# Mamba-2 scan written feature-major, with the gate projected like every other tile

## Chip, core and metric

One core of one Trainium2 chip runs the whole program: two blocks of a small language model over 512 tokens. The metric is the time of one execution on the device in microseconds, here the median of three runs. Engines are called as in the profile: PE (TensorE, PEld its weight load), DVE (VectorE), ACT (ScalarE), POOL (GpSimd), SP (SyncE, which issues nearly all DMAs).

## What is computed

Two layers, each feed-forward half, mixer, feed-forward half. The mixer of the first layer is a Mamba-2 scan, of the second a sliding-window attention. All operands are fp32. The part that matters here, cut from the reference (32 heads of 64 in 8 groups of 4 heads, state 128, chunk 128, so 4 chunks):

```python
z, xbc, dt = split(u @ w_in)
xs, B, C = split(silu(causal_conv4(xbc) + conv_b))
dt = softplus(dt + dt_bias);  a_cum = cumsum(dt * a)          # within a chunk
decay = exp(where(causal, a_cum_l - a_cum_s, -inf))
y_diag = einsum('bclgn,bcsgn->bgcls', C, B) * decay  @  (xs * dt)
states = B^T @ (exp(a_end - a_cum) * xs * dt), carried over chunks with exp(a_end)
y = y_diag + (C @ states_before) * exp(a_cum) + d_skip * xs
gg = y * silu(z);  gg = gg * rsqrt(mean(gg * gg, over the 256 of a group) + eps)
out = (gg * norm_w) @ w_out
```

## The kernel before

**Layout.** Activations lie feature-major: 128 features on the partitions, 512 tokens along the row. A product of fp32 precision is made of three matmuls on halves (`mm3`, L326: high weight by high x, high by low, low by high). `project` (L331) makes one tile of 128 features by 512 tokens out of 8x3 such matmuls with 512 columns each. For every weight tile ACT casts the loaded `wraw` to `whi` (L218), and another engine subtracts to get `wlo` (L219): DVE, or POOL where `split_w` is given it. `next_w` (L225) splits two tiles ahead and loads four ahead; there are two buffers for `wraw` and four for each half.

**Mamba.** `mamba` (L459) runs through `MAMBA_ORDER` (L45), a hand-written list of tokens, once for each of 8 groups g: `z` the gate, `B`, `C`, `X`, `Y` projections with their convolution (`conv`, L521: one multiplication from PSUM into `xp`, one ACT and three DVE passes of 128x512 into `acc`, a Silu), `h` the decay factors, `a b c f g` the five steps of the generator `ssd` (L557), and `O` the output projection of an earlier group, whose 128x512 results DVE adds to the residual `h` (L455). The tokens of neighbouring groups are interleaved, and each engine executes its own instructions in the order that a scheduler made of the program. PSUM has four one-bank buffers (`mm`) and two two-bank buffers (`big`).

In this kernel y is token-major. `z_first` (L631) and `z_next` (L649) therefore hold x still and move the weights: 96 matmuls of 256 columns (288 in the first group, which carries the 32 columns of dt along). `steps` and `steps_end` (L480, L505) turn dt into the step sizes, their cumulated sums `acs` and the exponentials `ee`, and send the transposed sums to DRAM (`actr`). `decay` (L538) fetches them as rows over all partitions, and subtracts `acs` with 16 DVE instructions of 128x128 (L552) ahead of an Exp. In `ssd`, token c makes x token-major by 8 transposes (`psx`), copies it (L574), and scales it three ways: `xds` on DVE (L576), `xd` and `y` on POOL (L578, L580). Token f multiplies: `psy` 16 products of a 128x128 stationary factor with 64 columns of `xd` (L600), `pso` with the state (L603); then come four DVE passes over y (L604 to L607), squares with their row sums on ACT (L610), a reciprocal root by Newton's method on DVE (`rsqrt`, L293), and its product into y (L616). Token g transposes y back (`psyt`, L621) into the halves `ya`, `yb` that `O` multiplies.

Of the kernel before, what the change touches and what calls it, by code (L numbers as in the profile page):

```python
# [84 lines left out]
def weight_plan():  # L85
# [18 lines left out]
    def mamba():  # L104
# [6 lines left out]
        for tok in MAMBA_ORDER:  # L111
            s, g, q = parse(tok)
            z = np.arange(256) + g * 256
            if tok == "z0":
                zd = np.concatenate([z, 6144 + np.arange(32)])
                for ks in (range(0, 3), range(3, 6), range(6, 8)):
                    cols_over_k(wi, ks, zd)
            elif s == "z":
                for ks in (range(0, 4), range(4, 8)):
                    cols_over_k(wi, ks, z)  # L120
            elif s in "BCXY":
                c0 = {"B": 4096 + g * 128, "C": 5120 + g * 128, "X": 2048 + g * 256, "Y": 2176 + g * 256}[s]
# [795 lines left out]
```

## Time and profile before

| | |
|---|---|
| median of 3 runs (lowest, highest) | 2076.58 us (2074.08 to 2076.80) |
| the profiled execution, its own time | 2076.16 us |
| its span in the trace | 2074.4 us, so 1.8 us lie outside |
| busy share PE, DVE, ACT, POOL | 99%, 53%, 36%, 8% |
| mean granted PE clock | 0.998 |
| chain that ended last, share by engine | PE 91%, DVE 6%, ACT 1%, others under 1% each |
| Mamba stage | from 370 us (first `psz`) to about 820 us |

Busy time is the union of an engine's instructions; matmuls overlap in the pipeline, so that an instruction's duration is longer than its distance to the next, and the distance is what adds up. Where a timeline row has a count (x24), it is one uninterrupted run of instructions. A wait row names the engine that waited, what it was to execute, and whose instruction released it.

### The profile page before, as it was taken

The numbers are of one execution on the slowest core, as the hardware profiler recorded it, in microseconds if no ns is written. First come the engines' busy times: TensorE is split into PE (matmuls) and PEld (weight loads), VectorE is DVE, ScalarE is ACT, GpSimd is POOL, SyncE is SP. The second block draws the span as 40 slices with busy tenths as digits, with TensorE's granted clock in tenths as the row PEclk, the third lists the DMA queues.
The fourth block names the chain that finished last, engine by engine and source line by source line (L and its number), as shares of the span: only waits on it lengthen the run. The fifth ranks groups of instructions, "written<-read, shape, count | busy, mean of one in ns | idle before, by whom it ended". The sixth has DMA issues, their size and how long they took to land.

```text
span 2074.4 us, 24948 instructions
## 1 busy us (share of the span) xinstructions
PE 2045.5 (99%) x9991; PEld 1717.8 (83%) x9991; DVE 1093.8 (53%) x1782; ACT 736.7 (36%) x1088; POOL 166.1 (8%) x120
## 2 busy tenths in 40 slices
PE   8999999999999999999999999999999999999998
PEld 7888888888888887888888888888887788888887
DVE  6343433687888889434333346343338884443333
ACT  5232222445444444322222233232226563232231
POOL 0000001222222210000001000000102000000000
PEclk9999999999999999999999999999999999999999
DMA  5333232323333332233333333322332223333231
GB/s 172 102 92 102 87 104 87 114 92 91 94 100 102 102 102 72 92 102 92 101 94 92 99 100 98 102 92 94 99 102 62 62 71 92 96 97 101 89 98 69
DMA packets 58869, 197.64 MB, mean 95 GB/s; under 512 B 6656, under 2 KB 6912, under 8 KB 58752
## 3 DMA queue, kind: packets, MB, share of 16 engines
q1 hardware_dynamic: 58608, 196.03, 30.6%
q8 instruction: 79, 1.29, 0.3%
q14 instruction: 38, 0.31, 0.0%
q10 hardware_dynamic: 144, 0.00, 0.0%
HBM read 193.85 MB, written 2.16 MB: 94 GB/s over the span
## 4 chain that ended last, share of the span: by engine, by line
PE 91%; DVE 6%; ACT 1%; issue 1%; DMA 1%; POOL 0%; ACTq 0%; SPq 0%; DVEq 0%; POOLq 0%
PE mm L327 27%; PE mm L328 27%; PE mm L329 27%; PE psz L658 1%; PE psz L660 1%; PE psz L659 1%; PE psy L600 1%; DVE acc L528 1%; DVE wlo L219 1%; PE pav L799 0%; PE pp L788 0%; ACT lg L775 0%; POOL qkv L742 0%; PE pso L603 0%; DVE lg L768 0%
## 5 line engine op out<-in xcount | busy, mean ns | idle before, releaser
L218 ACT CAST whi<-wraw 128x1024 fp32r<-128x1024 f32 (+2 forms) x355 | 364.8, 1030 | 1061.0 <-PE mm L328 677.3
L327 PE MATMUL mm<-x,whi 128*128 128x512 f32 x1760 | 690.2, 392 | 5.8 <-DVE whi L216 5.8
L329 PE MATMUL mm<-x,wlo 128*128 128x512 f32 x1760 | 685.7, 390 | 0.9 <-DVE wlo L219 0.9
L328 PE MATMUL mm<-x,whi 128*128 128x512 f32 x1760 | 685.8, 390 | 0.0
L219 DVE TENSOR_TENSOR wlo<-wraw,whi 128x1024 fp32r<-128x1024 f32 (+3 forms) x329 | 392.1, 1192 | 305.8 <-ACT whi L218 291.7
L327 PEld LDWEIGHTS mm<-x,whi 128*128 128x128 f32 x1760 | 331.0, 188 | 74.9 <-ACT ss L265 5.7
L329 PEld LDWEIGHTS mm<-x,wlo 128*128 128x128 f32 x1760 | 330.6, 188 | 70.8 <-DVE wlo L219 1.9
L328 PEld LDWEIGHTS mm<-x,whi 128*128 128x128 f32 x1760 | 331.1, 188 | 67.9
L327 PE MATMUL mm<-ga,whi 128*128 128x512 f32 (+1 forms) x726 | 277.9, 383 | 0.0
L328 PE MATMUL mm<-gb,whi 128*128 128x512 f32 (+1 forms) x726 | 277.7, 383 | 0.0
L329 PE MATMUL mm<-ga,wlo 128*128 128x512 f32 (+1 forms) x726 | 277.7, 383 | 0.0
L343 DVE TENSOR_TENSOR t<-mm,t 128x512 f32<-128x512 f32 x88 | 60.9, 692 | 270.1 <-PE mm L329 269.6
L341 DVE TENSOR_TENSOR t<-mm,rbc 128x512 f32<-128x512 f32 x88 | 60.5, 691 | 212.2 <-PE mm L329 212.1
L273 POOL TENSOR_TENSOR ss<-ss,sq 128x512 f32<-128x512 f32 x27 | 39.7, 1471 | 1512.3 <-ACT sq L269 1512.3
L327 PEld LDWEIGHTS mm<-ga,whi 128*128 128x128 f32 x726 | 136.5, 188 | 26.6
L328 PEld LDWEIGHTS mm<-gb,whi 128*128 128x128 f32 x726 | 136.5, 188 | 26.6
L329 PEld LDWEIGHTS mm<-ga,wlo 128*128 128x128 f32 x726 | 136.5, 188 | 26.5
L219 POOL TENSOR_TENSOR wlo<-wraw,whi 128x1024 fp32r<-128x1024 f32 x30 | 73.4, 2448 | 218.8 <-ACT whi L218 218.8
L528 DVE SCALAR_TENSOR_TENSOR acc<-xp,par,acc 128x512 f32<-128x512 f32 x96 | 85.5, 891 | 1.4 <-ACT acc L526 1.3
L658 PE MATMUL psz<-whi,x 128*128 128x256 f32 x224 | 65.5, 292 | 5.7 <-DVE xp L524 5.7
L455 DVE TENSOR_TENSOR h<-mm,h 128x512 f32<-128x512 f32 x88 | 59.2, 685 | 12.8 <-PE mm L329 12.6
L660 PE MATMUL psz<-whi,x 128*128 128x256 f32 x224 | 64.6, 288 | 0.0
(194 smaller groups left out, 1828.4 us busy)
## 6 DMA issues: line engine op xcount, KB each, us to landing
wraw<-wflat SPq DMA_DIRECT2D x320, 512.0 KB, 3.6
wraw<-wflat SPq DMA_DIRECT2D x32, 384.0 KB, 3.1
abc<-actr SPq DMA_DIRECT2D x32, 256.0 KB, 4.7
h<-xT SPq DMA_DIRECT2D x8, 256.0 KB, 4.5
out<-out SPq DMA_DIRECT2D x4, 512.0 KB, 2.6
wraw<-wflat SPq DMA_DIRECT2D x4, 256.0 KB, 2.9
wraw<-wflat SPq DMA_DIRECT2D x2, 432.0 KB, 3.3
cst<-consts SPq DMA_DIRECT2D x1, 321.5 KB, 5.1
```

Of the source, the lines that this page charges most:

```text
L218: act.copy(hi[:, :w], r[:, :w])
L219: (eng or dve).tensor_sub(lo[:, :w], r[:, :w], hi[:, :w].bitcast(F32))
L273: pool.tensor_add(norm["ss"], norm["ss"], sq)
L327: pe.matmul(ps, whi, xt[0], start=first, stop=False)
L328: pe.matmul(ps, whi, xt[1], start=False, stop=False)
L329: pe.matmul(ps, wlo, xt[0], start=False, stop=last)
L341: dve.tensor_mul(t, pg, rbc)
L343: dve.tensor_mul(t, pu, t)
L455: dve.tensor_add(h[m], ps, h[m])
L528: dve.scalar_tensor_tensor(acc, xp[:, j:j + S], pcol(P_CW + t * 4 + j), acc, op0=ALU.mult, op1=ALU.add)
L658: pe.matmul(pz, x[k][:, 0, ts], hi[:, sl], start=k == 0, stop=False)
L660: pe.matmul(pz, x[k][:, 1, ts], hi[:, sl], start=False, stop=k == KT - 1)
```

## The change

Y is kept feature-major through the scan. (1) The gate z is projected like every other tile (tokens Z and W, two per group); dt has a projection of its own, 32 features by 512 tokens, and four transposes to token-major (`dt_project`). (2) `psy` takes the 64 columns of `xd` as the stationary operand and moves the 128 columns of the decay factor; heads alternate between the two halves of the output partitions. `pso` likewise takes the state as stationary. (3) The factors exp(a_cum) are stored to DRAM (`eetr`) and fetched for every group as rows over 64 partitions each (`ee`, 4 DMAs). (4) The group's sum of squares is made by ACT squares, one DVE add and matmuls with a column of constants (`psg`, new token i after g); its reciprocal root `rn`, 128 tokens by 4 chunks, goes to a DRAM row as 512 single elements (`row`) and comes back over all partitions (`rb`); in the last group a spread by PE (`psb`) takes its place. (5) The transposes `psyt` and the copy `xtok` go. (6) The decay subtraction moves from DVE to ACT (Relu with scale -1, then Exp with scale -1). (7) POOL keeps nothing but the three-column memsets: all `wlo`, and `xd`, are DVE's.

```diff
-    o = ["z0", "d0", "B0", "e0", "C0", "X0", "h0", "Y0", "a0"]
+    o = ["Z0", "n0", "W0", "s0", "d0", "B0", "C0", "e0", "X0", "h0", "Y0", "a0"]
     for g in range(NG - 1):
         n = g + 1
         q = [f"O{g - 2}:{i}" for i in range(4)] if g >= 2 else [None] * 4
-        o += [f"z{n}", f"g{g - 1}" if g else None, f"b{g}", f"B{n}", f"c{g}", q[0], q[1], f"C{n}", f"h{n}",
-              q[2], q[3], f"f{g}", f"X{n}", f"Y{n}", f"a{n}"]
+        o += [f"Z{n}", f"g{g - 1}" if g else None, f"W{n}", f"b{g}", f"i{g - 1}" if g else None, f"B{n}", f"c{g}",
+              q[0], q[1], f"C{n}", f"h{n}", q[2], q[3], f"f{g}", f"X{n}", f"Y{n}", f"a{n}"]
     e = NG - 1
-    o += [f"O{e - 2}:0", f"O{e - 2}:1", f"g{e - 1}", f"b{e}", f"O{e - 2}:2", f"c{e}", f"O{e - 2}:3", f"f{e}",
-          f"O{e - 1}:0", f"O{e - 1}:1", f"O{e - 1}:2", f"O{e - 1}:3", f"g{e}",
+    o += [f"O{e - 2}:0", f"g{e - 1}", f"b{e}", f"O{e - 2}:1", f"i{e - 1}", f"c{e}", f"O{e - 2}:2", f"O{e - 2}:3",
+          f"f{e}", f"O{e - 1}:0", f"O{e - 1}:1", f"O{e - 1}:2", f"g{e}", f"O{e - 1}:3", f"i{e}",
           f"O{e}:0", f"O{e}:1", f"O{e}:2", f"O{e}:3"]
...
+        eetr = dram.tile([HEADS, CHUNKS, 128], F32, name="eetr")
+
+        def silu_z(ps, zs, j):
+            dve.tensor_mul(zs[:, j, :], ps, rbc)
+            act.activation(zs[:, j, :], zs[:, j, :], AF.Silu)
+
+        def dt_project():
+            ...
...
+            et = t2([128, 128], name="et")
+            act.activation(et, at, AF.Exp)
+            for c in range(CHUNKS):
+                nc.sync.dma_start(eetr[:, c, :], et[c * HEADS:(c + 1) * HEADS, :])
             pe.matmul(pt[:, 1, 0:128], sel, acs.rearrange(flat), start=True, stop=True)
             dve.tensor_sub(tb.rearrange(flat), pt[:, 1, 0:128], acs.rearrange(flat))
-            act.activation(ee, acs, AF.Exp)
...
+            e = m4([128, 2, S], name="ee")
+            for j in range(2):
+                for a in range(2):
+                    nc.sync.dma_start(e[64 * a:64 * a + 64, j, :],
+                                      eetr[g * 4 + 2 * j + a].rearrange("c l -> (c l)").unsqueeze(0)
+                                      .to_broadcast([64, S]))
             for u in range(2):
                 for c in range(2):
                     for r in range(4):
                         i = g * 4 + r
-                        dve.tensor_scalar(ab[u][:, c, r, :], ab[u][:, c, r, :],
-                                          acs[:, 2 * u + c, i:i + 1], 0.0, op0=ALU.subtract, op1=ALU.min)
-                act.activation(ab[u], ab[u], AF.Exp)
-            return ab
-
-        def ssd(g, ab, bc, xc, zs, pairs):
+                        act.activation(ab[u][:, c, r, :], ab[u][:, c, r, :], AF.Relu, scale=-1.0,
+                                       bias=acs[:, 2 * u + c, i:i + 1])
+                act.activation(ab[u], ab[u], AF.Exp, scale=-1.0)
+            return ab, e
...
-            xtok = m4([128, 4, 256], name="xtok")
-            act.copy(xtok, px)
+            xd = m4([128, 4, 256], name="xd")
+            dve.tensor_mul(heads(xd), heads(px), per_head(dtt, g))
             xds = m4([128, 4, 256], name="xds")
-            dve.tensor_mul(heads(xds[:, 0:3]), heads(xtok[:, 0:3]), per_head(dtds, g, 0, 3))
-            xd = m4([128, 4, 256], name="xd")
-            pool.tensor_mul(heads(xd), heads(xtok), per_head(dtt, g))
-            y = m4([128, 4, 256], name="y")
-            pool.tensor_mul(heads(y), heads(xtok), par[:, P_D + g * 4:P_D + g * 4 + 4].unsqueeze(1)
-                            .unsqueeze(3).to_broadcast([128, 4, 4, 64]))
+            dve.tensor_mul(heads(xds[:, 0:3]), heads(px[:, 0:3]), per_head(dtds, g, 0, 3))
...
-            py = big([128, 4, 256], name="psy")
+            py = big([128, 2, S], name="psy")
             for c in range(4):
                 for r in range(4):
-                    sl = slice(r * 64, (r + 1) * 64)
-                    pe.matmul(py[:, c, sl], ab[c // 2][:, c % 2, r, :], xd[:, c, sl], start=True, stop=True)
-            po = big([128, 4, 256], name="pso")
+                    hs = slice(r % 2 * 64, r % 2 * 64 + 64)
+                    pe.matmul(py[hs, r // 2, c * 128:(c + 1) * 128], xd[:, c, r * 64:(r + 1) * 64],
+                              ab[c // 2][:, c % 2, r, :], start=True, stop=True)
+            po = big([128, 2, S], name="pso")
             for c in range(1, 4):
-                pe.matmul(po[:, c, :], bc[:, 1, c * 128:(c + 1) * 128], st[:, c - 1, :], start=True, stop=True)
-            dve.tensor_add(y, py, y)
-            dve.tensor_mul(heads(xds[:, 1:4]), heads(po[:, 1:4]), per_head(ee, g, 1, 4))
-            dve.tensor_add(y[:, 1:4], y[:, 1:4], xds[:, 1:4])
+                for j in range(2):
+                    pe.matmul(po[:, j, c * 128:(c + 1) * 128], st[:, c - 1, j * 128:(j + 1) * 128],
+                              bc[:, 1, c * 128:(c + 1) * 128], start=True, stop=True)
+            y = m4([128, 2, S], name="y")
+            for j in range(2):
+                dve.scalar_tensor_tensor(y[:, j, :], xc[:, j, :], pcol(P_D + 2 * g + j), py[:, j, :],
+                                         op0=ALU.mult, op1=ALU.add)
+            dve.tensor_mul(e[:, :, 128:], po[:, :, 128:], e[:, :, 128:])
+            dve.tensor_add(y[:, :, 128:], y[:, :, 128:], e[:, :, 128:])
             dve.tensor_mul(y, y, zs)
-            sg = sm([128, 4], name="sg")
+            sq = [t2([128, S], name="sqy") for _ in range(2)]
+            for j in range(2):
+                act.activation(sq[j], y[:, j, :], AF.Square)
+            dve.tensor_add(sq[0], sq[0], sq[1])
+            yield
+            ps = mm([128, 4], name="psg")
             for c in range(4):
-                act.activation(xtok[:, c, :], y[:, c, :], AF.Square, accum_out=sg[:, c:c + 1])
+                pe.matmul(ps[:, c:c + 1], sq[0][:, c * 128:(c + 1) * 128], one, start=True, stop=True)
             v = sm([128, 4], name="gv")
-            dve.tensor_scalar(v, sg, 1.0 / 256.0, EPS, op0=ALU.mult, op1=ALU.add)
+            dve.tensor_scalar(v, ps, D / 256.0, EPS, op0=ALU.mult, op1=ALU.add)
             rn = sm([128, 4], name="rn")
             rsqrt(rn, v, 4, sm)
-            for c in range(4):
-                dve.tensor_scalar(y[:, c, :], y[:, c, :], rn[:, c:c + 1], None, op0=ALU.mult)
+            if g < NG - 1:
+                row = dram.tile([CHUNKS, 128], F32, name=f"row{g}")
+                nc.sync.dma_start(row.rearrange("c l -> l c"), rn)
+                rb = t2([128, S], name="rb")
+                nc.sync.dma_start(rb, row.rearrange("c l -> (c l)").unsqueeze(0).to_broadcast([128, S]))
             yield
+            if g == NG - 1:
+                rb = big([128, S], name="psb")
+                for c in range(4):
+                    pe.matmul(rb[:, c * 128:(c + 1) * 128], rn[:, c:c + 1].to_broadcast([128, 128]), ident,
+                              start=True, stop=True)
+            pairs += halves("y")
             for j in range(2):
-                pt = mm([128, S], name="psyt")
-                for c in range(4):
-                    pe.transpose(pt[:, c * 128:(c + 1) * 128], y[:, c, j * 128:(j + 1) * 128], ident)
-                if j == 0:
-                    pairs += halves("y")
-                yt = pairs[j]
+                dve.tensor_mul(y[:, j, :], y[:, j, :], rb)
                 w = pcol(P_NW + 2 * g + j)
-                act.activation(yt[0], pt, AF.Copy, scale=w)
-                dve.scalar_tensor_tensor(yt[1], pt, w, yt[0].bitcast(F32),
+                act.activation(pairs[j][0], y[:, j, :], AF.Copy, scale=w)
+                dve.scalar_tensor_tensor(pairs[j][1], y[:, j, :], w, pairs[j][0].bitcast(F32),
```

In `silu_z` (new) DVE multiplies the z tile by the token scale `rbc` and ACT applies Silu. Where the Mamba projections named `pool` for the subtraction of the low half, they now name nothing, so that DVE does it.

What this makes of DVE's order, first around token c of a steady group, behind the Newton steps of the group before it (`h_..` in later rows is the residual). Before:

```order
L219 TENSOR_TENSOR wlo<-wraw,whi 128x1024 x2
L627 SCALAR_TENSOR_TENSOR yb<-psyt,par,ya 128x512 x2
L576 TENSOR_TENSOR xds<-xtok,dtds 128x768
L524 TENSOR_TENSOR xp<-mm,rbc 128x512
L219 TENSOR_TENSOR wlo<-wraw,whi 128x1024
L528 SCALAR_TENSOR_TENSOR acc<-xp,par,acc 128x512
L593 TENSOR_TENSOR st<-st,cd 128x256
L528 SCALAR_TENSOR_TENSOR acc<-xp,par,acc 128x512
```

And now, with the semaphores waited for in brackets (DMAHW7 there is the DMA of `rb`):

```order
L467 TENSOR_TENSOR zs<-mm,rbc 128x512 [waits PE_49]
L214 TENSOR_TENSOR wlo<-wraw,whi 128x1024 [waits DMAHW4_49,Activation_49]
L586 TENSOR_TENSOR xd<-psx,dtt 128x1024 [waits PE_49]
L588 TENSOR_TENSOR xds<-psx,dtds 128x768
L646 TENSOR_TENSOR y<-y,rb 128x512 [waits DMAHW7_49]
L646 TENSOR_TENSOR y<-y,rb 128x512
L649 SCALAR_TENSOR_TENSOR yb<-y,par,ya 128x512 [waits Activation_49] x2
L530 TENSOR_TENSOR xp<-mm,rbc 128x512 [waits PE_49]
L600 TENSOR_TENSOR st<-st,cd 128x256 [waits Activation_49]
L214 TENSOR_TENSOR wlo<-wraw,whi 128x1024 [waits DMAHW5_49]
```

`yb` of the group before stood behind a wait for ACT alone; it now stands behind the product with `rb`, which waits for a DMA, and the next projection's `xp` and the state update `st` stand behind both.

SP's order in a steady group now (`rn` to DRAM is `row`, back is `rb`; the rest is weights, decay rows and `ee`):

```order
L197 DMA wraw<-wflat 128x1024 x6
L635 DMA row_5400<-rn 128x4x1
L637 DMA rb<-row_5400 128x512
L197 DMA wraw<-wflat 128x1024
L550 DMA abc<-actr 128x512 x2
L197 DMA wraw<-wflat 128x1024
L550 DMA abc<-actr 128x512 x2
L557 DMA ee<-eetr 64x512 x4
```

Before, the same queue held weights and `abc` alone; the store of `row` now waits for DVE's `rn` at the head of the queue, with `rb` and a weight load behind it.

DVE at the end of the stage, where group 6's product with `rb` stands between residual additions:

```order
L297 TENSOR_TENSOR rw_5824<-rw_5824,rn 128x4 [waits DVE_49]
L298 SCALAR_TENSOR_TENSOR rn<-rw_5824,rn 128x4 [waits DVE_49]
L450 TENSOR_TENSOR h_89<-mm,h_89 128x512 [waits PE_49]
L450 TENSOR_TENSOR h_90<-mm,h_90 128x512 [waits PE_49]
L646 TENSOR_TENSOR y<-y,rb 128x512 [waits DMAHW4_49]
L646 TENSOR_TENSOR y<-y,rb 128x512
L450 TENSOR_TENSOR h_91<-mm,h_91 128x512 [waits PE_49]
L649 SCALAR_TENSOR_TENSOR yb<-y,par,ya 128x512 [waits Activation_49] x2
```

and the end of the Newton steps of group 7, ahead of its last products:

```order
L450 TENSOR_TENSOR h_92<-mm,h_92 128x512 [waits PE_49]
L296 TENSOR_TENSOR rw_6029<-xh_6028,rn 128x4 [waits DVE_49]
L214 TENSOR_TENSOR wlo<-wraw,whi 128x1024 [waits DMAHW5_49,Activation_49]
L297 TENSOR_TENSOR rw_6029<-rw_6029,rn 128x4 [waits DVE_49]
L214 TENSOR_TENSOR wlo<-wraw,whi 128x1024 [waits DMAHW6_49,Activation_49]
L298 SCALAR_TENSOR_TENSOR rn<-rw_6029,rn 128x4 [waits DVE_49]
L296 TENSOR_TENSOR rw_6029<-xh_6028,rn 128x4 [waits DVE_49]
L297 TENSOR_TENSOR rw_6029<-rw_6029,rn 128x4 [waits DVE_49]
L298 SCALAR_TENSOR_TENSOR rn<-rw_6029,rn 128x4 [waits DVE_49]
L646 TENSOR_TENSOR y<-y,psb 128x512 [waits PE_49]
L646 TENSOR_TENSOR y<-y,psb 128x512
L649 SCALAR_TENSOR_TENSOR yb<-y,par,ya 128x512 [waits Activation_49] x2
```

Before, four products by `rn` (L616) stood where the products with `rb` and `psb` stand now, and waited for no DMA; the two `wlo` of the next stage stood behind the Newton steps.

## Rows read from the trace of the kernel before

**Rows 1.** The page's first part: busy time, share of the span, instructions of each engine.

```profile
PE 2045.5 (99%) x9991; PEld 1717.8 (83%) x9991; DVE 1093.8 (53%) x1782; ACT 736.7 (36%) x1088; POOL 166.1 (8%) x120
```

**Rows 2.** Busy time by stage: us, PE, PEld, DVE, ACT, POOL, PEclk, DMA share, GB/s.

```profile
434.00:487.00 53.00, 49.89 (x307) 45.22 (x306) 42.43 (x85) 26.90 (x41) 17.04 (x13) 0.97 0.31 94
487.00:540.00 53.00, 50.42 (x280) 44.43 (x279) 42.08 (x74) 23.88 (x37) 12.19 (x8) 0.97 0.27 80
540.00:594.00 54.00, 54.00 (x318) 47.90 (x316) 43.86 (x77) 24.82 (x39) 14.25 (x10) 1.00 0.33 102
```

**Rows 3.** Waits of PE, stretch 434:487: us in total, times, longest.

```profile
PE psz L658 <- DVE xp L524: 3.1, 1, 3.1
```

**Rows 4.** Timeline of DVE, 444:460: start us, us, engine, line, operation.

```profile
453.97 2.91 DVE L528 SCALAR_TENSOR_TENSOR acc<-xp,par,acc 128x512 f32<-128x512 f32 x1
...
456.88 0.68 DVE L524 TENSOR_TENSOR xp<-mm,rbc 128x512 f32<-128x512 f32 x1
```

**Rows 5.** Timeline of POOL, the same stretch.

```profile
451.15 5.19 POOL L219 TENSOR_TENSOR wlo<-wraw,whi 128x1024 fp32r<-128x1024 f32 x2 [12.97 <-ACT whi L218]
```

**Rows 6.** Busy time in the tail, columns as in rows 2.

```profile
768.73:805.42 36.69, 33.31 (x176) 27.55 (x174) 34.87 (x63) 11.90 (x23) 4.47 (x2) 1.00 0.13 45
```

**Rows 7.** Timeline of PE in the tail.

```profile
794.15 0.39 PE L327 MATMUL mm<-ya,whi 128*128 128x512 f32 x1
...
801.86 0.39 PE L328 MATMUL mm<-yb,whi 128*128 128x512 f32 x1
```

**Rows 8.** Timeline of PE, one steady group.

```profile
647.02 2.79 PE L600 MATMUL psy<-xd,abc 128*128 128x64 f32 x24
649.64 1.51 PE L603 MATMUL pso<-st,bc 128*128 128x256 f32 x6
650.81 0.58 PE L327 MATMUL mm<-x,whi 128*128 128x512 f32 x1
...
663.04 0.36 PE L658 MATMUL psz<-whi,x 128*128 128x256 f32 x1
...
674.63 1.03 PE L621 MATMUL psyt<-cst,y 128*128 128x128 f32 x8
```

**Rows 9.** Timeline of PE, the first group's z: first instruction, and the one after 72.

```profile
370.27 0.29 PE L644 MATMUL psz<-whi,x 128*128 128x288 f32 x1
...
379.78 0.95 PE L309 MATMUL psn<-cst,ss 128*128 128x1 f32 x8
```

**Rows 10.** Timeline of PE in the attention layer.

```profile
1657.79 0.39 PE L329 MATMUL mm<-oa,wlo 128*128 128x512 f32 x1
1658.11 1.75 PE L799 MATMUL pav<-pT,vtok 128*64 128x128 f32 x28
1659.79 1.42 PE L788 MATMUL pp<-cst,lg 128*128 128x128 f32 x11
```

**Rows 11.** Groups by line and form in the Mamba stage: xcount, busy us, mean ns, idle before.

```profile
L219 DVE TENSOR_TENSOR wlo<-wraw,whi 128x1024 fp32r<-128x1024 f32 x34 | 42.8, 1259 | 29.0 <-ACT whi L218 29.0
...
L552 DVE TENSOR_SCALAR abc<-abc,acs 128x128 f32<-128x128 f32 x128 | 34.1, 340 | 0.9 <-DMA abc<-actr 0.9
```

**Rows 12.** Timeline of DVE in the tail: six small operations of a reciprocal root.

```profile
768.02 0.16 DVE L301 TENSOR_TENSOR rw<-xh,rn 128x4 f32<-128x4 f32 x1
...
769.20 1.14 DVE L616 TENSOR_SCALAR y<-y,rn 128x256 f32<-128x256 f32 x4
```

**Rows 13.** DMA issues: tensors, queue, xcount, KB each, median us to landing.

```profile
abc<-actr SPq DMA_DIRECT2D x32, 256.0 KB, 4.7
...
wraw<-wflat SPq DMA_DIRECT2D x4, 256.0 KB, 2.9
...
actr<-at SPq DMA_DIRECT2D x1, 64.0 KB, 1.6
par<-params ACTq DMA_DIRECT2D x1, 4.0 KB, 3.0
```

More of the change, by code (lines that the diff above doesn't have):

```diff
@@ L40 @@
 P_D = P_AL + 32
-P_SK = P_D + 32
+P_SK = P_D + 16
 NPAR = P_SK + 16
@@ L112, in mamba @@
             s, g, q = parse(tok)
[L113 to L122, printed above, removed]
+            if s == "d":
+                cols_over_k(wi, range(KT), 6144 + np.arange(32))
+            elif s in "ZWBCXY":
+                c0 = {"Z": g * 256, "W": g * 256 + 128, "B": 4096 + g * 128, "C": 5120 + g * 128,
+                      "X": 2048 + g * 256, "Y": 2176 + g * 256}[s]
                 cols_over_k(wi, range(KT), c0 + np.arange(128))
@@ L469, in mamba @@
         acs = sm(rowp, name="acs", bufs=1)
-        ee = sm(rowp, name="ee", bufs=1)
         cd = sm(rowp, name="cd", bufs=1)
         actr = dram.tile([128, 128], F32, name="actr")
-        def z_evac(pz):
-            zs = m4([128, 4, 256], name="zs")
+        eetr = dram.tile([HEADS, CHUNKS, 128], F32, name="eetr")
[3 more added lines that the diff above has]
+        def dt_project():
+            hi, lo = next_w()
+            ps = mm([128, S], name="psd")
+            for k in range(KT):
+                sl = slice(k * 32, k * 32 + 32)
+                mm3(ps[0:32, :], hi[:, sl], lo[:, sl], (x[k][:, 0, :], x[k][:, 1, :]), k == 0, k == KT - 1)
+            part = t2([32, S], name="dtp")
+            act.copy(part, ps[0:32, :])
+            pz = mm([128, 4, 32], name="psdt")
             for c in range(4):
-                act.activation(zs[:, c, :], pz[c][:, 0:256], AF.Silu, scale=rcol[:, c:c + 1])
-            return zs
+                pe.transpose(pz[:, c, :], part[:, c * 128:(c + 1) * 128], ident[0:32, 0:32])
+            return pz
         def steps(pz):
@@ L649, in z_next @@
-        def z_next():
-            ws = [next_w(pool), next_w(pool)]
-            zs = m4([128, 4, 256], name="zs")
-            for c in range(4):
-                pz = mm([128, 256], name="psz")
-                ts = slice(c * 128, (c + 1) * 128)
-                for k in range(KT):
-                    hi, lo = ws[k // 4]
-                    sl = slice(k % 4 * 256, (k % 4 + 1) * 256)
-                    pe.matmul(pz, x[k][:, 0, ts], hi[:, sl], start=k == 0, stop=False)
-                    pe.matmul(pz, x[k][:, 0, ts], lo[:, sl], start=False, stop=False)
-                    pe.matmul(pz, x[k][:, 1, ts], hi[:, sl], start=False, stop=k == KT - 1)
-                act.activation(zs[:, c, :], pz, AF.Silu, scale=rcol[:, c:c + 1])
-            return zs
+        held = []
@@ L666, in mamba @@
             s, g, q = parse(tok)
-            if tok == "z0":
-                pz = z_first()
-                zss[0] = z_evac(pz)
-            elif s == "z":
-                zss[g] = z_next()
+            if s in "ZW":
+                j = "ZW".index(s)
+                if j == 0:
+                    zss[g] = m4([128, 2, S], name="zs")
+                ps = project()
+                if g == 0:
+                    held.append(ps)
+                else:
+                    silu_z(ps, zss[g], j)
+            elif s == "n":
+                rcol = token_scale(big, [norm["ss"]], 0, 4)
+            elif s == "s":
+                rbc = spread(rcol)
+                for j in range(2):
+                    silu_z(held[j], zss[0], j)
             elif s == "d":
-                tatb = steps(pz)
+                tatb = steps(dt_project())
             elif s == "e":
```

32 lines of the change are left out of this document (7 added, 25 removed).

## The prediction

> **What bounds the kernel now.** I read the page's first part before anything else: PE is busy for 99% of the span, DVE for half of it, so a saved matmul is worth its time wherever PE does not wait, and work taken off another engine is worth nothing unless PE waits for that engine [rows 1]. Next the stages. From 540 us on PE has no idle time in a group (54.00 of 54), while DVE has 43.86 and ACT 24.82 [rows 2]. The two stretches before it are not full: 3.1 and 2.6 us idle, and the granted clock is 0.97 of its upper level of 2.4 GHz in both [rows 2]. The waits say who is late: PE, about to start a z tile, waits for the DVE multiplication `xp` [rows 3]. The timelines say why DVE is late: a 128x512 pass that lasts 2.91 us, where one a little later has 0.68 [rows 4], lies beside two POOL subtractions that together take 5.19 us [rows 5]. So POOL's work slows DVE while it runs, and only in these two places, in the groups that have no output projection between their parts yet, does PE feel it. The profiled execution took 2076.2 us, 0.4 under the median of the three runs; the sum is made against it. About 0.2%, 4 us, can be told from no change.
>
> **PE's own work, outside the tail.** I call tail what follows the last projection, from 768.73 to the first matmul of the last output projection at 805.42 [rows 6].
>
> - z in groups 1 to 7: now 48 matmuls of 512 columns, each (801.86 - 794.15) / 34 = 0.227 behind the one before [rows 7], 10.88; before, 96 of 256 columns from 663.04 to 674.63, 11.59 [rows 8]. Seven times -0.71: -5.0.
> - First group: 72 matmuls of 288 columns took 379.78 - 370.27 = 9.51, or 0.132 each, 96 of them 12.7 [rows 9]. Now 10.88 for z, 24 x 0.227 = 5.44 for dt (a tile with 32 features has as many columns to move as one with 128), four transposes of about 0.11: 16.8. And PE executes in order, so the transposes wait for ACT's copy of the dt tile, one 512-column pass of about 0.7. Together +4.8.
> - `psy`: 24 instructions in 649.64 - 647.02 = 2.62, 0.109 each, 32 of them 3.49 a group [rows 8]. With 64 stationary and 128 moving columns on alternating output halves the nearest row is the attention product: 28 in 1.68, 0.06 each [rows 10], so 1.92. Before this run PE needed 1658.11 - 1657.79 = 0.32 from the last ordinary matmul [rows 10], against 0.227 between ordinary ones [rows 7]: 0.1 more. I take 2.02, or -1.47. The Trainium skill (TensorEngine Tiling (Array Packing), Key Properties) says that a change of the tiling mode drains TensorE; this speaks against the change, the 0.1 agrees with it, and it is the whole price here.
> - `pso`: 6 of 256 columns in 1.17 [rows 8]; now 12 of 128 columns at `psy`'s old 0.109, 1.31: +0.14. With `psy` -1.33, in seven groups -9.3.
> - `psyt`'s 8 transposes go and `psg`'s 8 instructions with a 128-wide weight load come. Runs of 8 of either kind lasted 1.03 and 0.95 [rows 8, 9]: nothing.
>
> Sum: -5.0 + 4.8 - 9.3 = **-9.5**.
>
> **The early stalls.** They cost 3.1 + 2.6 idle, and 3% of some 100 us of work at the lower clock, 3.0 [rows 2]. With POOL empty, no DVE operation is drawn out. DVE's own load: it gains four `wlo` a group at 1.26, but loses 16 decay subtractions at 0.34 [rows 11]; with `xd`, two z products, two `rb` products and a square sum in, the row scalings out and the POOL delays gone, it stays at about 42 in a group in which PE has some 52 of work (the third stage row, less 2). ACT gains 16 small passes, at DVE's 0.34 at most 5.4, on 24.82. Neither becomes the bound. I take the whole **-8.7**; the ends are that and 0.
>
> **The new wait for rb.** In each of five steady groups, with time zero at `psg`: `rn` is ready after 4.6 (13 small DVE operations, two of them behind a `wlo` and a z product, at (769.20 - 768.02) / 6 = 0.20 each [rows 12]). PE meanwhile makes `psg` (0.9), the W tile (5.4) and `psx` (0.9), DVE then `xd` and `xds` (together some 3), so that DVE reaches its first product with `rb` at about 10.2. Then `row` must have been stored and `rb` loaded. For the load the nearest rows are 2.9 (256 KB) and 4.7 (256 KB repeated from DRAM rows, in several transfers at a time) [rows 13]. For a store of 512 pieces of 4 bytes there is no row: a 64 KB store took 1.6, a load in 128 pieces of 32 bytes 3.0 [rows 13]. I take 3.0, because it is the row of small pieces; the far end adds its 1.4 over the store once per 128 pieces, 1.6 + 4 x 1.4 = 7.2. So `rb` lands between 9.1 and 16.5, and with 3.0 and 2.9 at 10.5, 0.3 late. What queues behind it on DVE is `yb`, the next `xp` and the state additions, which free the PSUM buffers that PE's output projection needs next; PE so waits about what DVE waits, and 0.2 more. Five times 0.5: **+2.5** (0 to +33). The weight loads behind the store on SP's queue cost nothing: their `wraw` buffers come free later anyway. The four `ee` DMAs of a group are issued at token h and used at token f behind the next group's projections, and 4.7 is the longest comparable row.
>
> The Trainium skill (DMA: Bandwidth & Descriptors, Rules for kernel authors) says that a transfer whose last dimension is not contiguous becomes one descriptor per element, and its Specifications that below 512 bytes the engine reads, modifies and writes. No row here shows what that costs for a store; by this rule the far end is the better guess.
>
> **The tail.** Before, 36.7 us, in which PE is busy for 33.3 [rows 6]; now 33.3 - 1.33 + 0.88 for `psb` (8 instructions at 0.11), 32.9. To it come PE's waits, worked out from the order of DVE: `xd` is made by DVE behind both products with the decay factors, PE's `psy` waits 2.0; the residual additions stand behind the product with group 6's `rb`, and PE's output tiles behind them, 3.6; the squares and their sum ahead of `psg`, 1.6; group 7's root has 13 x 0.2, two `wlo` at 1.26 [rows 11] and two additions of 0.7 between its steps, 6.4, of which 2.7 are covered by one output part of 12 matmuls, 3.7; then `psb`, product and cast, 1.5. Sum 32.9 + 12.4 = 45.3, **+8.6** (ends: +3 where two of the waits overlap, +14 with a lower clock behind the gaps, of which the early stalls gave 3.0).
>
> **Sum.** 2076.2 - 9.5 - 8.7 + 2.5 + 8.6 = 2069.1; I say **2069**.
>
> **The rivals.**
> 1. *The store of row is slow* (slower). The place is DVE's wait for `rb`, five times, and once in the tail. Each us over 3.0 costs 6; at 4.2 all the gain is gone, from 4.9 on it is measurably slower, at 6.0 it gives 2069 + 18 = 2087. For it: 512 pieces are more than any row here has in so small a transfer, and the store sits in a queue with large loads. Against it: 128 pieces of 32 bytes took no longer (3.0) than 256 KB (2.9) [rows 13], so pieces as such seem cheap.
> 2. *The early stalls stay* (same). Then 2078. For it: DVE's load is about 42 with or without POOL, and a group without output projection is only some 54 - 48 x 0.227 = 43 long. Against it: the drawn-out operations lie exactly beside POOL [rows 4, 5].
> 3. *The halves of psy don't overlap*, so the change does not do there what it says: 32 at 0.109 again, 7 x 1.57 = 11 more, 2080. Against it: the attention product has the same form and has 0.06 [rows 10].
> 4. *All waits are covered*: `rb` in time, tail +3. 2069 - 2.5 - 5.6 = 2061. For it: in the tail the waits were added up one behind the other, and some will overlap.
>
> **How the numbers follow.** Forecast 0.40, between 2064 and 2075; rival 1 0.23, rival 2 0.10, rival 3 0.08, rival 4 0.17, leaving 0.02. Faster by over 0.2% is below 2072.4: most of the forecast's interval (0.30) and rival 4, with a little of the others, 0.50. Slower is above 2080.7: rival 1 but for its lower edge, some of rivals 2 and 3, 0.27. The rest, 0.23, is within 0.2%. The range reaches from below rival 4 to rival 1 at 6 us: 2058 to 2088. The likeliest case alone has 2064 to 2075.
>
> **What would show it.** Right: PE without a wait between 430 and 540 us and a granted clock of 1.00 there; `psy` 32 in about 2.0; z tiles at 0.227 per matmul; the store of `row` about 3 us to landing, and DVE's idle time ahead of the `rb` product below 1 us; the tail some 45 us, with waits of PE for `xd`, for additions behind `rb`, and for `psb`. Wrong: waits of PE for additions or `xp` behind `rb` of several us in every group (rival 1); waits at z or W tiles in the first groups (rival 2); `psy` at 0.11 each (rival 3). A steady group should be about 1.5 us shorter.

## The result: slower, and where the time went

The changed kernel took 2141.12 us in the median of 4 runs (2140.36 to 2142.20), the one before 2075.82 (2074.08 to 2076.80): a ratio of 1.0315, 95% interval 1.0302 to 1.0328. The profiled execution has a span of 2139.1 us, 64.7 more. First the page, with its answer to [rows 1] and a DMA line, and from the list of all DMAs the store (tensors, queue, count, KB each, median us to landing):

```profile
PE 2055.1 (96%) x9691; PEld 1696.6 (79%) x9691; DVE 1080.0 (50%) x1708; ACT 765.0 (36%) x1149; POOL 59.2 (3%) x74
...
rb<-row SPq DMA_DIRECT2D x7, 256.0 KB, 5.2
```

```profile
row<-rn SPq DMA_DIRECT2D x7, 2.0 KB, 8.6
```

The store of `row` takes 8.6 us, and the load of `rb` 5.2; the sum had 3.0 and 2.9. The waits of PE in the whole Mamba stage (total, times, longest), and the longest of DVE:

```profile
PE mm L322 <- ACT st L598: 29.8, 4, 7.7
PE mm L322 <- DVE h L450: 12.5, 3, 10.8
PE mm L322 <- DVE xp L530: 6.8, 1, 6.8
PE pso L612 <- ACT st L598: 6.3, 1, 6.3
```

```profile
DVE y L646 <- DMA rb<-row: 60.1, 7, 10.5
```

DVE stands 60.1 us before its product with `rb`, in seven places and up to 10.5 at a time. The waits of PE above are what follows from it: `st`, `xp` and the residual additions `h` are queued behind that product. By stretch (us, PE, PEld, DVE, ACT, POOL, PEclk, DMA share, GB/s), against [rows 2]:

```profile
434.00:470.00 36.00, 36.00 (x202) 30.28 (x201) 30.38 (x51) 25.35 (x40) 0.30 (x3) 1.00 0.46 135
470.00:511.00 41.00, 33.01 (x170) 27.53 (x168) 26.12 (x38) 21.43 (x38) 0.40 (x4) 0.88 0.49 104
...
613.97:675.65 61.68, 53.99 (x271) 44.39 (x270) 42.07 (x67) 27.07 (x45) 0.40 (x4) 0.94 0.34 98
830.00:868.00 38.00, 20.75 (x85) 16.42 (x85) 23.31 (x45) 8.16 (x11) 0.00 (x0) 0.76 0.21 63
```

The first of them is where the early stall was: 36.00 of 36 at a clock of 1.00. Then come a stretch with 8.0 us idle, a like one, and steady groups of about 61.7 us with 7.7 idle and a mean clock of 0.94. The last row lies in the tail. One steady group in four timelines, of DVE, SP, ACT and PE (start, us, engine, line, operation):

```profile
704.40 0.95 DVE L588 TENSOR_TENSOR xds<-psx,dtds 128x768 f32<-128x768 f32 x1
712.57 1.29 DVE L646 TENSOR_TENSOR y<-y,rb 128x512 f32<-128x512 f32 x2 [7.21 <-DMA rb<-row]
```

```profile
699.06 0.38 SPq L635 DMA_DIRECT2D row<-rn  x1
706.75 0.33 SPq L637 DMA_DIRECT2D rb<-row  x1
```

```profile
713.29 1.33 ACT L648 ACTIVATE ya<-y,par 128x512 fp32r<-128x512 f32 x2 [10.66 <-DVE y L646]
...
715.47 0.36 ACT L598 COPY st<-psst 128x256 f32<-128x256 f32 x1
```

```profile
715.88 0.80 PE L322 MATMUL mm<-ya,whi 128*128 128x512 f32 x1 [7.02 <-ACT st L598]
```

SP issues the store at 699.06, and can issue the load when it has landed, at 706.75. `rb` arrives at 712.5; DVE, done with `xds` at 705.35, has waited 7.2 us. Then ACT makes `ya`, a cast and `st`, which frees the PSUM buffer that PE has waited for since 708.9.

Marks in the two traces give the whole difference. To the first matmul of z: 370.3 and 369.5 us. From there to the last group's first `psc`, the start of the tail: 398.5 and 441.4, **+42.9**. Tail, to the first matmul of the last output projection: 36.7 and 56.4, **+19.7**. The rest: 1269.0 and 1271.8, +2.8, which begins at a clock below 1.00 (0.60 in its first 7.7 us).

### The profile page after: what moved, and what is told of

Read it like the earlier page. It is cut to its first block, busy times and chain, and to the rows that moved or that the text cites. A ratio compares the mean times of both kernels' runs of the same rounds, so it can differ in the third digit from the quotient of the medians.

```text
span 2139.1 us, 24345 instructions
## 1 busy us (share of the span) xinstructions
PE 2055.1 (96%) x9691; PEld 1696.6 (79%) x9691; DVE 1080.0 (50%) x1708; ACT 765.0 (36%) x1149; POOL 59.2 (3%) x74
## 4 chain that ended last, share of the span: by engine, by line
PE 84%; DVE 5%; DMA 5%; ACT 2%; issue 2%; POOL 0%; SPq 0%; ACTq 0%; DVEq 0%; POOLq 0%
PE mm L322 27%; PE mm L323 27%; PE mm L324 27%; DMA row<-rn 3%; DMA rb<-row 2%; DVE wlo L214 1%; ACT whi L213 1%; DMA abc<-actr 1%; PE pav L799 1%; PE pso L612 1%; PE pp L788 1%; DVE acc L534 1%; PE psy L607 0%; POOL qkv L742 0%; DVE y L646 0%
## 5 line engine op out<-in xcount | busy, mean ns | idle before, releaser
L213 ACT CAST whi<-wraw 128x1024 fp32r<-128x1024 f32 (+1 forms) x355 | 365.2, 1030 | 1120.8 <-PE mm L323 698.0
L322 PE MATMUL mm<-x,whi 128*128 128x512 f32 x1888 | 741.5, 393 | 5.7 <-ACT x L278 5.7
L324 PE MATMUL mm<-x,wlo 128*128 128x512 f32 x1888 | 736.6, 390 | 0.4 <-DVE wlo L214 0.4
L323 PE MATMUL mm<-x,whi 128*128 128x512 f32 x1888 | 736.0, 390 | 0.0
L214 DVE TENSOR_TENSOR wlo<-wraw,whi 128x1024 fp32r<-128x1024 f32 (+3 forms) x359 | 427.5, 1192 | 288.4 <-ACT whi L213 271.2
L322 PEld LDWEIGHTS mm<-x,whi 128*128 128x128 f32 x1888 | 355.4, 188 | 79.4 <-ACT x L278 5.7
L324 PEld LDWEIGHTS mm<-x,wlo 128*128 128x128 f32 x1888 | 354.9, 188 | 75.5 <-DVE wlo L214 1.2
L323 PEld LDWEIGHTS mm<-x,whi 128*128 128x128 f32 x1888 | 355.6, 188 | 72.7
L322 PE MATMUL mm<-ya,whi 128*128 128x512 f32 x128 | 58.2, 460 | 50.7 <-ACT st L598 29.8
L322 PEld LDWEIGHTS mm<-ya,whi 128*128 128x128 f32 x128 | 27.5, 216 | 61.0 <-ACT st L598 31.4
L534 DVE SCALAR_TENSOR_TENSOR acc<-xp,par,acc 128x512 f32<-128x512 f32 x96 | 71.6, 748 | 3.2 <-ACT acc L532 2.7
L342 DVE TENSOR_TENSOR gb<-t,ga 128x512 fp32r<-128x512 f32 x88 | 60.3, 685 | 2.1 <-ACT ga L341 2.1
```

The source lines that it names most:

```text
L213: act.copy(hi[:, :w], r[:, :w])
L214: (eng or dve).tensor_sub(lo[:, :w], r[:, :w], hi[:, :w].bitcast(F32))
L322: pe.matmul(ps, whi, xt[0], start=first, stop=False)
L323: pe.matmul(ps, whi, xt[1], start=False, stop=False)
L324: pe.matmul(ps, wlo, xt[0], start=False, stop=last)
L342: dve.tensor_sub(gs[i][1], t, gs[i][0].bitcast(F32))
```

## The experiments

**What makes the store slow.** Theory A: its 512 single elements. Theory B: the weight loads on the same queue. `e4_actq` issues the store from ACT's queue:

```diff
-                nc.sync.dma_start(row.rearrange("c l -> l c"), rn)
+                nc.scalar.dma_start(row.rearrange("c l -> l c"), rn)
```

> The changed kernel with the store of row issued by ACT's queue, where no weight load is queued; the rb load stays on SP's. Theory A: the store keeps 8 to 9 us, the time about 2141 (ACT may lose a little while it waits for rn). Theory B: the store lands in about 3 us, DVE's wait for rb falls by some 5 us in each of 7 places, and the time to about 2100.

```profile
row<-rn ACTq DMA_DIRECT2D x7, 2.0 KB, 8.5
```

2139.69 us, and 8.5 for the store: B falls. The trace of the changed kernel says the same. Its last store, issued at 824.10 in the tail, has no other transfer beside it (DMA share 0.00 and 0 GB/s), and it is one of the slowest. First the stretch behind its first 2 us, columns as before, then its time to landing:

```profile
826.00:835.50 9.50, 3.26 (x12) 2.02 (x12) 0.69 (x1) 0.00 (x0) 0.00 (x0) 0.84 0.00 0
```

```profile
DMA to landing us min/median/max: 11.3/11.3/11.3
```

`e1_rowt` stores four pieces of 512 bytes (it also has a token of its own for the transposition, not shown):

```diff
+                pr = mm([128, 128], name="psr")
+                pe.transpose(pr[0:4, :], rn, ident)
+                rt = t2([128, 128], name="rt")
+                dve.tensor_copy(rt[0:4, :], pr[0:4, :])
...
-                nc.sync.dma_start(row.rearrange("c l -> l c"), rn)
+                nc.sync.dma_start(row, rt[0:4, :])
```

> The changed kernel, but rn (128 tokens by 4 chunks) is first transposed by PE to 4 rows of 128 and copied by DVE, so that the row is stored as 4 pieces of 512 bytes and not as 512 single elements; one more PE instruction and one more small DVE copy a group. Theory A (the store of 8.6 us is slow because of its 512 single elements): the store lands in 1.6 to 2.9 us, as the 64 KB and the 16 KB stores of 512-byte pieces do, the rb load stays at 5.2; the store is issued some 2.5 us later than in the changed kernel, so rb lands about 4 us earlier, the wait of DVE for rb falls from 60 us in 7 waits to about 30, and the time to about 2110. Theory B (the store waits behind the weight loads on SP's queue): the store keeps about 8 us, and the time rises by the later issue to 2150 or more.

SP's timeline shows the issue of the store and, behind its landing, that of the load; then DVE's wait for `rb`:

```profile
622.11 0.27 SPq L640 DMA_DIRECT2D row<-rt  x1
...
623.79 0.37 SPq L642 DMA_DIRECT2D rb<-row  x1
```

```profile
DVE y L651 <- DMA rb<-row: 11.2, 5, 2.8
```

1.7 us from issue to issue here (1.2 to 3.7 in the seven places), the wait down from 60.1 to 11.2 us, and 2084.86 in one run: some 56 us from the form of one store, more than the 30 expected. Is it the number of pieces? `e8_pieces` (on `e7_gate`, below) splits the store into four DMAs of 128 elements:

```diff
+                for c in range(CHUNKS):
+                    nc.sync.dma_start(row[c:c + 1, :].rearrange("c l -> l c"), rn[:, c:c + 1])
```

> e7_gate with the store of row as four DMAs of 128 single elements (one chunk each) one behind the other on SP's queue, to see how the time of a store goes with its pieces; the wait for them is hidden there, so the time should not tell (2073). Theory A (the time is the elements', one after another on the rings): the first of the four lands after some 3 to 4 us, the last after 8 to 9, the median near 6. Rival (a fixed cost of a store with a transposed pattern): each of the four takes about 8 us or more.

The 20 stores took 7.1 to 8.8 us, 8.1 in the median (2075.39 in all): about 8 for each of the four, as the rival has it, and not 3 to 9 one behind the other. `e11_probe` adds stores that nothing reads:

```diff
+            n = (4, 1, 2, 3, 4, 1, 0, 0)[g]
+            if n:
...
+                nc.sync.dma_start(probe[0:n, :].rearrange("c l -> l c"), rn[:, 0:n])
+            elif g == 6:
...
+                nc.sync.dma_start(flat4, rn)
```

> The kernel with the spread by PE in every group (e2_psb) and, beside it, one store of rn to DRAM a group that nothing reads, of 512, 128, 256, 384, 512 and 128 single elements of 4 bytes in groups 0 to 5, and of 128 pieces of 16 bytes in group 6; nothing waits for them, so the time stays near 2077. Theory A (the time goes with the number of pieces): about 3 to 3.5 us for 128, 5 for 256, 7 for 384, 8.5 for 512, and 3 to 3.5 for the 16-byte pieces. Rival (a fixed cost of a transposed store or of writing less than some size): 128 single elements take 7 us or more as well.

```profile
probe<-rn SPq DMA_DIRECT2D x2, 2.0 KB, 9.9
probe<-rn SPq DMA_DIRECT2D x2, 0.5 KB, 7.5
...
flat<-rn SPq DMA_DIRECT2D x1, 2.0 KB, 1.4
```

128 single elements take 7.5 already, four times as many 9.9 (medians of two each), and 128 pieces of 16 bytes 1.4: theory A falls in the form I gave it. The number is not what counts. `e12_probe2` has 128 pieces in every store and changes their size and distance (`step` elements from piece to piece, `n` written):

```diff
+                name, step, n = (("adj", 1, 1), ("gapp", 4, 1), ("gapq", 16, 1), ("gapr", 128, 1),
+                                 ("two", 2, 2), ("four", 4, 4), ("adjb", 1, 1))[g]
+                probe = dram.tile([128, step], F32, name=name)
+                nc.sync.dma_start(probe[:, 0:n], rn[:, 0:n])
```

> As e11_probe, with stores of 128 pieces each, one a group, that nothing reads: single elements of 4 bytes side by side (adj, group 0, and adjb, group 6), 16 bytes apart (gapp), 64 bytes apart (gapq), 512 bytes apart (gapr), then pieces of 8 bytes side by side (two) and of 16 bytes side by side (four). The run before showed that 128 single elements side by side take 7.5 us and 128 pieces of 16 bytes 1.4, so the number of pieces is not what costs. Theory S (a piece of 4 bytes is slow as such): adj and all three gaps take about 7, two is in between, four 1.4. Theory N (single elements are slow because neighbours are written into the same stretch of memory): adj takes 7, the gaps fall with the distance, gapr to about 1.5 to 2.

```profile
adj<-rn SPq DMA_DIRECT2D x1, 0.5 KB, 8.2
gapp<-rn SPq DMA_DIRECT2D x1, 0.5 KB, 2.3
gapq<-rn SPq DMA_DIRECT2D x1, 0.5 KB, 1.7
gapr<-rn SPq DMA_DIRECT2D x1, 0.5 KB, 1.9
two<-rn SPq DMA_DIRECT2D x1, 1.0 KB, 3.0
four<-rn SPq DMA_DIRECT2D x1, 2.0 KB, 2.9
adjb<-rn SPq DMA_DIRECT2D x1, 0.5 KB, 7.2
```

Theory S falls, and the gaps do what theory N said: 4-byte elements side by side take 8.2 and 7.2, the same elements 16 bytes or more apart 1.7 to 2.3. The place in the program is not the reason: in group 1 the two probe runs have 7.0 for 128 elements side by side and 2.3 for the same 16 bytes apart, in group 6 they have 1.4 for 16-byte pieces and 7.2 for 4-byte ones. Theory N's reason is not shown, though, as pieces of 8 and 16 bytes have neighbours as well and take 3.0 and 2.9. Each length stands on one or two stores. (The probes are not free: 2081.25 and 2081.91 against 2077.23 without them.)

**Is the wait all?** `e2_psb` spreads `rn` by PE in every group:

```diff
-            if g < NG - 1:
-                row = dram.tile([CHUNKS, 128], F32, name=f"row{g}")
...
             yield
-            if g == NG - 1:
-                rb = big([128, S], name="psb")
+            rb = big([128, S], name="psb")
```

> The changed kernel without any trip of rn through DRAM: every group spreads rn by PE into PSUM (8 instructions, 0.88 us) as the last group does already. Theory W (the whole loss is the wait for rb, with the lower clock behind each stall): outside the tail 9.5 us of PE work saved less 6 x 0.88, early stalls gone (8.7), tail some 5 us longer than before: about 2069, a steady group 52.3 us with the clock at 1.00. Rival (the feature-major order itself costs, through ACT or DVE queues or table loads): PE waits for st, h or xp remain in the steady groups without rb, and the time stays above 2085.

2077.23 us, ratio to the kernel before 1.0008 (0.9999 to 1.0018): the 64 us are gone, and no PE wait over 0.6 is left outside start and tail, but it is 8 more than expected. The steady group has 53.33 us without a gap, where 52.3 were expected. PE's timeline shows most of it: `psy` is executed in three runs a group (as before), and each now changes the stationary operand from 128*128 to 128*64 and back.

```profile
625.96 0.39 PE L324 MATMUL mm<-ya,wlo 128*128 128x512 f32 x1
626.28 0.43 PE L607 MATMUL psy<-abc,xd 128*64 128x128 f32 x2
626.64 0.50 PE L322 MATMUL mm<-ya,whi 128*128 128x512 f32 x1
626.98 0.39 PE L323 MATMUL mm<-yb,whi 128*128 128x512 f32 x1
```

```profile
641.11 1.74 PE L607 MATMUL psy<-abc,xd 128*64 128x128 f32 x26
642.78 1.60 PE L612 MATMUL pso<-bc,st 128*128 128x128 f32 x12
```

Two instructions here occupy 626.98 - 625.96 = 1.02 us together with one ordinary matmul before and one behind, which alone take 2 x 0.227: 0.57 for 2 instructions, against 0.13 at the pitch. The long run has 1.67 for 26 and 0.1 ahead; the other short one (4 instructions), by the same reckoning, 0.58. So `psy` costs 2.9 us a group, and not 2.02.

`e3_late` was to hide the trip by a later token i (only the tokens around it are shown):

```diff
-    f"b{g}", f"i{g - 1}" if g else None, f"B{n}", f"c{g}", q[0], q[1], f"C{n}",
+    f"b{g}", f"B{n}", f"c{g}", q[0], q[1], f"i{g - 1}" if g else None, f"C{n}",
```

> The changed kernel with token i (the product with rb) moved behind the output parts O:0 and O:1, some 12 us later in a steady group and 6.5 us later in the first two; the DMAs are untouched. Theory W: the store stays at 8.6 us and the load at 5.2, but no steady group waits for them: groups of about 51.5 us at clock 1.00; the tail is unchanged (56 us), so about 2085. Rival (the stall comes from SP's queue, where the weight loads stand behind the store and the rb load): the waits turn into waits for weights (whi or wlo), and the time stays above 2115.

```profile
701.42 1.29 DVE L646 TENSOR_TENSOR y<-y,rb 128x512 f32<-128x512 f32 x2 [7.47 <-DMA rb<-row]
```

2128.12 us, and DVE still waits 7.47: in the order that the scheduler made, the product still stands right behind `xds`; only the casts moved. So the run didn't test what it was made for; that it is 13 us faster is shorter waits of PE (for `st`, `xp` and `h` together 44 us instead of 57). `e7_gate` holds the product by data, with a scalar operand of one that is computed from the residual behind output part O:1 (the lines that leave groups 0, 6 and 7 without the trip and move token i are not shown):

```diff
+                gate1 = sm([128, 1], name="gate1")
+                dve.tensor_scalar(gate1, h[3][:, 0:1], 0.0, 1.0, op0=ALU.mult, op1=ALU.add)
...
+                    dve.scalar_tensor_tensor(y[:, j, :], y[:, j, :], gate1, rb, op0=ALU.mult, op1=ALU.mult)
```

> The changed kernel with its trip through DRAM kept in groups 1 to 5 (single elements, SP's queue), but the product with rb made to come later on DVE by data: its scalar operand is a one computed from the residual that output part O:1 has just written, and token i stands behind that part. Groups 0, 6 and 7 spread by PE. Theory W (the loss was DVE standing in front of a DMA that takes 14 us, nothing else): store and load keep 8 and 5 us, no PE wait remains in groups 2 to 6, a steady group has 0.9 us less than in e2_psb, 52.4, and the time is about 2072. Rival (SP's queue: weight loads behind the store and behind the rb load come late): waits for whi or wlo appear in each of these groups, and the time stays above 2085.

```profile
rb<-row SPq DMA_DIRECT2D x5, 256.0 KB, 5.7
...
row<-rn SPq DMA_DIRECT2D x5, 2.0 KB, 8.2
```

```profile
532.32 1.68 PE psy L607 x26
...
584.78 1.67 PE psy L607 x26
```

2073.19 in one run: store and load as slow as ever (8.2 and 5.7), groups of 52.4 us from `psy` to `psy`, and no wait of PE in them, for weights neither. Theory W holds. A group with the same work took 61.7 in the changed kernel, of which 7.7 was idle; the remaining 1.5 goes with the lower clock behind the stall (0.94 in the mean of a group, where `e2_psb` has 1.00).

**The early stalls and the tail.** `e5_before_dve` makes one part of the change in the kernel before, the low halves on DVE:

```diff
-                conv(project(pool), 24 + g, bcs[g][:, 1, :])
+                conv(project(), 24 + g, bcs[g][:, 1, :])
...
-            ws = [next_w(pool), next_w(pool)]
+            ws = [next_w(), next_w()]
```

(and token Y alike).

> The kernel before with one part of the change alone: all low halves of the weights are subtracted on DVE; POOL keeps the two products xd and y. Theory P (the early stalls of 3.1 and 2.6 us, with 3.0 of lower clock, come from POOL's subtractions drawing DVE out): both stalls go and the clock is 1.00 there, about 2067. Rival (DVE as such is late in the groups without an output projection; with four more subtractions of 1.26 it has some 48 of 53 us in a steady group): the stalls stay or grow, 2075 or more.

```profile
434.00:487.00 53.00, 53.00 (x323) 47.56 (x323) 44.35 (x87) 28.23 (x45) 4.68 (x6) 1.00 0.26 80
487.00:540.00 53.00, 53.00 (x311) 47.02 (x310) 42.58 (x80) 25.03 (x39) 4.68 (x6) 1.00 0.33 101
```

```profile
PE psyt L621 <- DVE y L616: 3.6, 1, 3.6
```

2069.43, ratio 0.9972 (0.9961 to 0.9983): both stretches of [rows 2] are full at a clock of 1.00, and no pass like the drawn-out one of [rows 4] is left (at most 0.75 us for any of its line, where the kernel before had up to 2.93). But in the tail PE now waits 3.6 for the last scaled y. DVE's timeline there:

```profile
793.11 1.22 DVE L219 TENSOR_TENSOR wlo<-wraw,whi 128x1024 fp32r<-128x1024 f32 x1
...
794.32 1.22 DVE L219 TENSOR_TENSOR wlo<-wraw,whi 128x1024 fp32r<-128x1024 f32 x1
795.45 1.13 DVE L616 TENSOR_SCALAR y<-y,rn 128x256 f32<-128x256 f32 x4
```

Two `wlo` of the next stage stand between the last steps of the root, as in the changed kernel. `e9_dve_late` (on this kernel) and `e10_gate_late` (on `e7_gate`) hold these two by data (from `y` in the first, from `rn` in the second):

```diff
+                one1 = sm([128, 1], name="one1")
+                dve.tensor_scalar(one1, y[:, 3, 0:1], 0.0, 1.0, op0=ALU.mult, op1=ALU.add)
...
+            dve.scalar_tensor_tensor(lo[:, :w], r[:, :w], one1, hi[:, :w].bitcast(F32),
+                                     op0=ALU.mult, op1=ALU.subtract)
```

> The kernel before with the low halves on DVE (e5_before_dve), and with the first two low halves of the next stage made to come behind the last group's root, by data: they are multiplied by a one computed from the last scaled y. Theory: the 3.65 us that PE waits there for y come from these two subtractions (2.4) standing between the root's steps, which the change shares; without them the wait is about 1.2 and the clock stays up behind it, about 2066. Rival: the root itself with the residual additions is what PE waits for, and the time stays 2069.

> e7_gate (round trip hidden in groups 1 to 5, spread in groups 0, 6, 7) with the same hold on the first two low halves of the next stage. Theory: PE's wait for rn ahead of psb falls from 3.8 to about 1.4 and the clock behind it stays up, so about 2069. Rival: the clock drop and the wait stem from the products and casts behind psb, 2072 or more.

```profile
PE psyt L630 <- DVE y L621: 1.6, 1, 1.6
```

```profile
PE psb L647 <- DVE rn L303: 1.9, 2, 1.7
```

2067.12, ratio 0.9963 (0.9949 to 0.9977), and 2070.76, ratio 0.9978 (0.9969 to 0.9988). Both beat the kernel before, and the first, which has nothing of the new layout, is the fastest of all. `e6_tail` gives the tail another order of tokens (written out here with their numbers):

```diff
-    O5:0 g6 b7 O5:1 i6 c7 O5:2 O5:3 f7 O6:0 O6:1 O6:2 g7 O6:3 i7 O7:0 ...
+    b7 O5:0 g6 c7 O5:1 f7 i6 O5:2 O5:3 O6:0 O6:1 g7 O6:2 O6:3 i7 O7:0 ...
```

> The kernel with the spread by PE in every group (e2_psb), with another order of the tokens behind the last projection: token f of the last group stands ahead of two more output parts, and two parts instead of one lie between its psg and its psb. Theory: the excess of that kernel over the one before lies in the tail (44.3 us instead of 36.7, and 2.1 of lower clock behind it); with 5.4 instead of 2.7 us of output matmuls beside the last root, PE's wait for rn falls from 3.75 to about 1 and the clock stays up, so about 2072 to 2074. Rival: PE waits for xd and xds instead at the earlier psy, and nothing is won (2077).

```profile
PE psx L584 <- ACT xc L536: 3.2, 2, 2.8
PE mm L322 <- ACT ya L642: 2.4, 1, 2.4
...
PE psy L607 <- DVE xd L586: 1.3, 1, 1.3
```

2077.16, one run: the wait for `rn` is gone, and waits for `xc`, `xd` and `ya` have come; nothing won, as the rival had it.

## Why the prediction was wrong

- **The new wait for rb** is the step that failed, with the two durations it took: "I take 3.0, because it is the row of small pieces" for the store measured 8.6 in the median (7.5 to 12.3), and 2.9 for the load 5.2, where the other end, 4.7, was the row of the same kind (a repeated read of DRAM rows). The row of 3.0 was a load, and it stood for a store. The mechanism was right: DVE reached its product 10.7 us behind `psg` (10.2 in the sum), `rb` came at 17.9, and PE waited about what DVE waited, 7.0 of 7.2. Even the far end of the store, 7.2, was too low. It was built on the number of pieces, and 128 pieces alone take 7.0 to 8.2.
- The places: I counted five groups and the tail; group 0, for which I had no term, waits 9.8 us as well. Nor was there a term for the clock, 1.5 us a group behind the stalls, though the early stalls had shown such a loss. With these the +42.9 ahead of the tail adds up, as an estimate: 44.6 of PE waiting in six groups, 6 x 1.5 for the clock, -8.7 for the early stalls and -2.4 of PE's own work (below) make 42.5.
- **Rival 1** was what happened, with its place right. Neither of its reasons is what the runs show (the count of pieces, the queue with large loads), and its price was too low: 6 us for each us of the store, by which 8.6 gives 2069 + 34 = 2103, and with the load 2.3 later in six places 2116.
- **PE's own work**: -9.5 was too much. A group without the trip has 52.4 us, 1.0 less than 53.4, where the sum had 2.0. `psy` saves 0.6 and not 1.5: 0.1 was taken for the change of the tiling mode, once a group, while the three runs take 0.44, 0.32 and 0.1 us more than their instructions at the pitch. The Trainium skill's rule that I weighed there (TensorEngine Tiling (Array Packing), Key Properties: a change of the mode drains) agrees with these rows; the price that I gave it was wrong. The first group's +4.8 was right: from the first matmul of z to group 0's first `psc` it is 38.4 us before and 43.0 now. With seven groups at -1.0 that is about -2.4, where -9.5 stood.
- **The early stalls**: right. They go with POOL's subtractions alone (`e5_before_dve`), and with the tail mended that kernel has 8.1 us less (`e9_dve_late`), where 8.7 were summed.
- **The tail**: +8.6 was predicted, with 3.6 of waiting behind group 6's `rb`. With the trip it is 56.4 us, +19.7, as the wait for the additions behind `rb` is 10.8 and not 3.6. Without the trip it is 44.3 instead of 36.7, +7.6 (`e2_psb`, row below), but that this is near 8.6 is luck in part: the 3.6 for `rb` is not in it, PE waits 8.1 us there instead of 12.4, and it is busy for 36.3 instead of 32.9, at a clock of 0.91.

```profile
761.83:806.15 44.32, 36.32 (x198) 29.75 (x196) 36.70 (x73) 10.88 (x16) 0.00 (x0) 0.91 0.19 60
```

- **The halves of psy**: they do overlap, 0.064 each; rival 3 falls.

The Trainium skill's rule on single elements (DMA: Bandwidth & Descriptors, Rules for kernel authors) spoke for the far end, and so better than the row that I preferred. What these runs show beside it is that the distance between the elements decides: 128 elements of 4 bytes took 1.9 us at 512 bytes apart.

Of the new layout as such, with the trip hidden, what is left is 2073.19 in one run, about the lowest run of the kernel before (2073.41); `e10_gate_late` has -4.5 us, while the two subtractions and POOL's relief bring -8.1 without it. So the layout gives nothing here: `e10_gate_late` is 3.6 us above `e9_dve_late` in the median, with ranges that overlap by half a microsecond. What the layout saves, 1.0 us a group, goes into a tail that is still 42.2 us long in `e10_gate_late` (36.7 before, 37.4 in `e9_dve_late`), and into the first group with its separate dt projection, 4.6 us longer than before.

## What to carry to other kernels

Before a value goes through DRAM to get spread over partitions, cost the store by its pattern: elements of 4 bytes side by side, one from each partition, cost 7 to 12 us here; behind a small transpose the store took 1.2 to 3.7 from its issue to that of the load. Where a scheduler orders an in-order engine, a late transfer costs all that is queued behind its consumer; moving the code in the program need not move it on the engine, a data dependence does. And when a change has several parts, try each alone: here one of them was worth more than the whole.

## What was not expected of the hardware

- Stores of 4-byte elements side by side: 7.0 to 8.2 us for 128 in the probe runs, 8.8 and 11.0 for 512 there and 7.5 to 12.3 in the changed kernel, 11.3 with no other transfer under way; 16 bytes apart 2.3, 64 apart 1.7, 512 apart 1.9; pieces of 8 bytes side by side 3.0, of 16 bytes 1.4 and 2.9. What makes 4-byte neighbours slow was not tried.
- A repeated read of a 2 KB row over 128 partitions took 5.2 to 5.8 us in the changed kernel's four steady groups, where a plain load of the same 256 KB had 3.0. The repetition by itself is not the price: in group 0 and in the tail the same read took 3.2 and 3.3, in group 1 4.0. What adds 2 us in the steady groups stays open.
- After a stall of 7 us PE ran mostly at the lower of its two levels (1.2 and 2.4 GHz) for a while: a granted clock of 0.56 in the 4 us behind the wait that ended at about 532 in the changed kernel, 1.00 in the 9 after that.

```profile
532.00:536.00 4.00, 3.48 (x9) 2.81 (x10) 4.00 (x8) 2.50 (x7) 0.07 (x1) 0.56 0.62 123
536.00:545.00 9.00, 9.00 (x57) 6.88 (x56) 6.05 (x10) 7.93 (x17) 0.10 (x1) 1.00 0.46 118
```
